# Two mixers in one transformer kernel: MoBA heads in pairs, row broadcasts through DRAM, and new SBUF addresses

## The chip, the cores and the metric

One core of one Trainium2 chip runs one program. The metric is the device time in microseconds of one execution; lower is better.

## What is computed

The reference is two transformer blocks of one layer each, in float32, on one sequence of 256 tokens of width 1024. Cut to what matters here:

```python
# first block
h = rmsnorm(x, norm_mix_pre)
proj = h @ w_in                                   # queries, keys, values, gates of three mixers
ya = gla_mixer(...) @ w_branch_a
yb = pool_mixer(...) @ w_branch_b
yc = moba_mixer(mq, mk, mv) @ w_branch_c          # 8 heads of width 64, causal attention with a
                                                  # linear bias; one block of 256 keys, so no selection
mixed = gs0 * ya + gs1 * yb + gs2 * yc            # gs = sigmoid(gates)
x = x + rmsnorm(mixed @ w_out);  x = x + rmsnorm(ffn(rmsnorm(x)))
# second block: three scans instead
y_hg = hgrn2_scan(...)                            # 8 heads of width 128
h_ml = mlstm_scan(q, k, v, i_pre, log_f)          # 4 heads; weights exp(bh[t] - bh[s] + ih[s] - m[t])
y_ssd = ssd_scan(xs, dt, A, Bm, Cm)               # 16 heads; weights exp(cum[t] - cum[s])
mixed = g0 * (y_hg @ w_br_hg) + g1 * (y_ml @ w_br_ml) + g2 * (y_mb @ w_br_mb)
x = x + mixed @ w_out;  x = x + ffn(rmsnorm(x));  return rmsnorm(x)
```

The scans are computed over all 256 tokens at once, as masked products, and not chunk by chunk.

## The kernel before

**Weights and precision.** All weights stream from HBM in pieces of 128 x 2048 words, one load each on SyncE's queue (two raw buffers, `wr`). ScalarE rounds each piece to float32r (`wh`), VectorE subtracts to get the rest (`wl`); there are three buffers of each. Every large product is three float32r matmuls: high by high, high by low, low by high (`three`). The normed input is held the same way, as `hhi` and `hlo`. Projections whose result is wanted channel-major (`proj_cm`) hold the weights stationary and move 256 tokens; those wanted token-major (`proj_tm`) hold the input stationary and move 512 weight columns. Their results are written to PSUM tiles `pp`; a piece is 48 matmuls of 256 columns or 24 of 512. `fetch` issues the loads and splits of a piece two pieces ahead of its use.

**Background work.** The mixers are Python generators. After each piece, `tick` advances every running generator to its next `yield`, so a mixer's small matmuls (PSUM tiles `m`, four banks) stand on TensorE between two weight pieces, one step a tick. They are plain float32, which TensorE does in two records each, with a transpose as one. TensorE works in the order in which the program is written, with few exceptions; VectorE and ScalarE are reordered by the scheduler that builds the program. Generators started earlier tick first.

**MoBA** (`moba`) runs next to the last projections and the gates of block 1. For head h, `scores` multiplies 64 channels of q and k (heads of even number lie on partitions 0 to 63, odd ones on 64 to 127, of one tile) into one bank: 128 columns for the first 128 queries, 256 for the rest. VectorE adds the bias and takes the row maxima, ScalarE the exponentials with their sums, VectorE divides. `turn` transposes the three 128 x 128 blocks and ScalarE copies them out. `values` multiplies by v, 64 output channels, into half of the partitions of a bank that two heads share. The loop runs `values(i - 2)`, `turn(i - 1)`, `scores(i)` in one tick, ten ticks for eight heads.

**mLSTM and SSD** (`mlstm`, `ssd`) run in block 2, mLSTM next to the projections for the output gate and SSD's input, SSD next to the gates and branches h and m. `rows` makes the running sums with time along the row, one head per partition, splits them into high and low parts in one tile `rowB`, and transposes another copy into columns. For each head `row_bc` then broadcasts one row to all partitions by a matmul: the stationary operand is one column of the 0/1 matrix `selr`, spread to 128, the moving one `rowB`, 256 columns. `causal_w` adds the column value to that PSUM tile, takes the minimum with a mask and then the exponential, in a 384-wide SBUF tile (`w1(384)`, four buffers that MoBA, mLSTM and SSD share). SSD handles two heads in a tick, and multiplies each head's weights with the inputs one tick later. A head's three products in mLSTM have 257 columns, in SSD 64.

**Addresses.** A partition of SBUF is one range of bytes; the address modulo 128 is called the residue below. Pools are laid out one after another in the order in which they are opened: constants, weights, big buffers, work tiles. The weight buffers are 2144 words (67 x 128 bytes) and all begin at residue 32. The ten big buffers (`b8`) are 2056 words, that is 64 x 128 + 32 bytes, so each begins 32 further than the one before it: 32, 64, 96, 0 and so on. `hhi` and `hlo` are the first two work tiles and begin at 96. A row of 256 tokens is 1024 bytes, so a slice keeps its tile's residue. The branch inputs Y, the split activations of the FFN and a few split weight pieces (`BIG`) lie in big buffers: Y of branch c at 64, b at 32, a at 64, h and m at 0 and 64, s at 0 and 96; of the `BIG` pieces that the FFN begins with, one at 96 and one at 32.

**POOL's queue** carries a few memsets, single-column powers, and loads: the bias, the pooling weights and the gains.

Of the kernel before, what the change touches and what calls it, by code (L numbers as in the profile page):

```python
# [8 lines left out]
F32 = mybir.dt.float32  # L9
# [7 lines left out]
T = 256  # L17
# [9 lines left out]
NBIG = 10  # L27
PP = 4
# [14 lines left out]
def _const_arrays():  # L43
# [16 lines left out]
    sel = np.zeros((128, 20))  # L60
    for h in range(4):
        sel[h, h] = sel[32 + h, h] = -1.0
    for h in range(16):
        sel[64 + h, 4 + h] = sel[96 + h, 4 + h] = 1.0
    parts["sel"] = sel
# [73 lines left out]
PW = 2144  # L139
PIECES = []  # L140
# [93 lines left out]
class Prog:  # L234
    def __init__(self, ctx, tc, A):
# [3 lines left out]
        self.wp = e(tc.tile_pool(name="wp", bufs=3))  # L239
        self.big = e(tc.tile_pool(name="big", bufs=NBIG))  # L240
        self.wk = e(tc.tile_pool(name="wk", bufs=2))
        self.pp = e(tc.tile_pool(name="pp", bufs=PP, space=bass.MemoryType.PSUM))
        self.mx = e(tc.tile_pool(name="mx", bufs=8 - PP, space=bass.MemoryType.PSUM))
# [16 lines left out]
    def b8(self, dt=F32, w=2048):  # L260
        return self.big.tile([128, 2056], dt, tag="b8", name=self.name("b"))[:, :w]
# [72 lines left out]
    def setup(self):  # L334
# [5 lines left out]
        self.selr = self.cp.tile([128, 20], F32R, name="selr")  # L340
# [7 lines left out]
        self.ident = self.c("ident")  # L348

# [53 lines left out]
    def load_consts(self):  # L403
        self.act(self.selr, self.c("sel"))
# [12 lines left out]
    def buffers(self, n):  # L417
# [4 lines left out]
        return (raw, *(self.wp.tile([128, PW], F32R, tag=g, name=f"{g}{n}", bufs=WBUF[g]) for g in ("wh", "wl")))  # L422
# [198 lines left out]
    def new_h(self):  # L621
        def one(nm):
            t = self.wk.tile([128, 2048], F32R, tag=nm, name=self.name(nm), bufs=1)
            return t.rearrange("p (k t) -> p k t", k=KT)
        return one("hhi"), one("hlo")
# [151 lines left out]
    def moba(self, q, k, v, alibi, OH, OL):  # L777

        nc = self.nc
        prob, turned, po = {}, {}, {}  # L780
        two = (slice(0, 128), slice(128, 384))

        def scores(h):
            c, p, slope = h // 2, slice(64 * (h % 2), 64 * (h % 2) + 64), 2.0 ** -(h + 1)
            sc = self.ps()
            self.mm(sc[:, 0:128], q[p, c, 0:128], k[p, c, 0:128])
            self.mm(sc[:, 128:384], q[p, c, 128:256], k[p, c, 0:256])
            s = self.w1(384)
            m = self.w1(8)
            self.tt(s, sc[:, :384], alibi, ALU.add)  # L790
            for t in range(2):
                nc.vector.tensor_reduce(out=m[:, t:t + 1], in_=s[:, two[t]], axis=AX.X, op=ALU.max)
# [739 lines left out]
```

## Time and profile before

| | us |
|---|---|
| median of 3 runs | 1058.92 |
| lowest, highest | 1057.8, 1063.15 |
| profiled execution, whole | 1060.68 |
| its span, first to last instruction | 1058.4 |
| TensorE (PE) busy | 1042.7 |
| VectorE (DVE) busy | 752.7 |
| ScalarE (ACT) busy | 605.8 |
| GpSimd (POOL) busy | 18.1 |
| granted TensorE clock, mean | 0.997 of full speed |

An engine's busy time is the time in which at least one of its instructions is open. TensorE's matmuls overlap, and their ends are modelled, so the busy share is not a share of its peak; the distance from one start to the next is what a matmul costs. Times in the rows are from the start of the span.

### The profile page before, as it was taken

The page shows a single profiled execution, that of the slowest core. Times are in us where ns is not written, and L with a number is a line of the kernel's source. Part 1 is how long each engine was busy: PE and PEld are TensorE (multiplying, and loading weights), DVE is VectorE, ACT ScalarE, POOL GpSimd, SP SyncE. Part 2 cuts the span into 40 slices and gives each one's busy share as a digit, 9 for nine tenths or more (in the row PEclk, how much of TensorE's full clock was granted, in tenths as well). Part 3 has the DMA queues.
Part 4 walks back from the last instruction along what each step waited for, and adds up shares of the span by engine and source line. Part 5 has one row for each costly group of instructions (what it writes and reads, how often), then busy time and mean ns, then how long its engine had stood idle before and what let it go on. Part 6 is the DMA issues. An engine that isn't in the chain of part 4 may idle for free.

```text
span 1058.4 us, 21256 instructions
## 1 busy us (share of the span) xinstructions
PE 1042.7 (99%) x8768; PEld 970.3 (92%) x8768; DVE 752.7 (71%) x1472; ACT 605.8 (57%) x1265; POOL 18.1 (2%) x29
## 2 busy tenths in 40 slices
PE   8999999999999999999989999999999999999997
PEld 7898899989999988799879899999999989999885
DVE  5766677687655545766888879977776686999753
ACT  7656455466554435655458656754565566776542
POOL 1000000001000000200000000000000000000000
PEclk9999999999999999999999999999999999999999
DMA  8643345555555546455425344454445554555561
GB/s 307 228 174 131 121 160 200 173 192 206 187 200 181 207 158 210 159 200 202 139 106 199 127 153 165 166 194 153 160 149 195 191 202 173 172 204 192 181 214 40
DMA packets 29936, 187.13 MB, mean 177 GB/s; under 512 B 3472, under 2 KB 4768, under 8 KB 8848
## 3 DMA queue, kind: packets, MB, share of 16 engines
q1 hardware_dynamic: 28544, 181.13, 49.0%
q0 software_dynamic: 720, 3.60, 0.9%
q8 instruction: 68, 1.11, 0.4%
q10 hardware_dynamic: 576, 1.05, 0.3%
q14 instruction: 28, 0.23, 0.1%
HBM read 184.72 MB, written 1.05 MB: 176 GB/s over the span
## 4 chain that ended last, share of the span: by engine, by line
PE 94%; DVE 2%; DMA 1%; ACT 1%; issue 1%; POOL 0%; SPq 0%; POOLq 0%; DVEq 0%; ACTq 0%
PE pp L298 86%; PE m L298 6%; DMA wr<-w 1%; DMA x<-x 1%; PE m L550 1%; DVE b L287 1%; PE m L617 0%; PE m L806 0%; POOL k L569 0%; ACT junk L564 0%; DVE wl L287 0%; ACT wh L284 0%; PE m L977 0%; DVE k L290 0%; ACT b L284 0%
## 5 line engine op out<-in xcount | busy, mean ns | idle before, releaser
L287 DVE TENSOR_TENSOR wl<-wr,wh 128x512 fp32r<-128x512 f32 (+2 forms) x660 | 424.2, 680 | 188.1 <-ACT wh L284 97.8
L284 ACT ACTIVATE wh<-wr 128x512 fp32r<-128x512 f32 (+2 forms) x660 | 373.3, 617 | 303.2 <-PE pp L298 273.6
L298 PE MATMUL pp<-hhi,wh 128*128 128x256 f32 x1440 | 199.9, 280 | 1.1 <-ACT hhi L284 1.0
L298 PE MATMUL pp<-hlo,wh 128*128 128x256 f32 x1440 | 194.8, 277 | 0.9 <-issue 0.9
L298 PE MATMUL pp<-hhi,wl 128*128 128x256 f32 x1440 | 194.2, 277 | 0.0
L298 PEld LDWEIGHTS pp<-hhi,wh 128*128 128x128 f32 x1440 | 180.0, 188 | 4.3 <-ACT hhi L284 2.1
L298 PEld LDWEIGHTS pp<-hlo,wh 128*128 128x128 f32 x1440 | 178.2, 188 | 1.1 <-issue 1.1
L298 PEld LDWEIGHTS pp<-hhi,wl 128*128 128x128 f32 x1440 | 178.1, 189 | 0.0
L298 PE MATMUL pp<-wh,b 128*128 128x512 f32 x512 | 131.2, 395 | 1.6 <-ACT wh L284 1.6
L298 PEld LDWEIGHTS pp<-wh,b 128*128 128x128 f32 x512 | 95.5, 188 | 24.4 <-ACT wh L284 1.7
L298 PE MATMUL pp<-b,wh 128*128 128x256 f32 x576 | 76.5, 282 | 0.0
L290 DVE SCALAR_TENSOR_TENSOR k<-pp,vecs,k 128x255 f32<-128x255 f32 (+1 forms) x148 | 70.2, 477 | 5.1 <-ACT k L284 3.7
L298 PEld LDWEIGHTS pp<-b,wh 128*128 128x128 f32 x576 | 71.6, 189 | 0.1
L298 PE MATMUL pp<-wl,b 128*128 128x512 f32 x256 | 71.3, 395 | 0.0
L298 PEld LDWEIGHTS pp<-wl,b 128*128 128x128 f32 x256 | 48.1, 188 | 11.4
L298 PE MATMUL pp<-wh,hhi 128*128 128x512 f32 (+3 forms) x232 | 52.4, 355 | 0.0
L298 PE MATMUL pp<-wh,hlo 128*128 128x512 f32 (+3 forms) x232 | 50.6, 348 | 0.0
L298 PE MATMUL pp<-wl,hhi 128*128 128x512 f32 (+3 forms) x232 | 50.4, 347 | 0.0
L298 PEld LDWEIGHTS pp<-wh,hlo 128*128 128x128 f32 x232 | 37.9, 188 | 6.1
L298 PEld LDWEIGHTS pp<-wl,hhi 128*128 128x128 f32 x232 | 37.9, 188 | 5.9
L284 ACT ACTIVATE k<-pp,vecs 128x256 f32<-128x256 f32 x62 | 34.4, 557 | 13.5 <-DVE k L290 8.7
L298 PEld LDWEIGHTS pp<-wh,hhi 128*128 128x128 f32 x232 | 37.0, 188 | 5.4 <-ACT k L284 0.3
(178 smaller groups left out, 929.3 us busy)
## 6 DMA issues: line engine op xcount, KB each, us to landing
wr<-w SPq DMA_DIRECT2D x158, 1024.0 KB, 4.8
wr<-w SPq DMA_DIRECT2D x10, 512.0 KB, 4.1
wr<-w SPq DMA_DIRECT2D x10, 256.0 KB, 4.7
wr<-w SPq DMA_DIRECT2D x2, 1072.0 KB, 4.9
wr<-w SPq DMA_DIRECT2D x2, 1056.0 KB, 4.9
b<-gains POOLq DMA_DIRECT2D x2, 1024.0 KB, 6.6
b<-xt SPq DMA_DIRECT2D x8, 128.0 KB, 4.3
x<-x SPq DMA_DIRECT2D x2, 512.0 KB, 6.7
```

The costliest lines, as they stand in the source:

```text
L284: return self.nc.scalar.activation(out=out, in_=in_, func=func, **k)
L287: return self.nc.vector.tensor_tensor(out=out, in0=a, in1=b, op=op)
L290: return self.nc.vector.scalar_tensor_tensor(out=out, in0=a, scalar=s, in1=b, op0=op0, op1=op1)
L298: return self.nc.tensor.matmul(out, lhsT=lhsT, rhs=rhs, start=start, stop=stop)
L550: self.nc.tensor.transpose(ps[:, k], part[:, 128 * k:128 * k + 128], self.ident)
```

## The change

**MoBA** works on pairs of heads. `scores(c)` issues the 256-column products of both heads one after the other, one on rows 0 to 63 and one on rows 64 to 127, each into its own bank, then the two 128-column ones. VectorE and ScalarE take the two heads in turn: both additions, then maxima and exponentials of each head, then the two divisions. `values(c)` alternates in the same way between the two halves of the output partitions. The loop has `values(i - 1)` and `scores(i)` in one tick and `turn(i)`, six transposes, in the next: nine ticks.

**Rows** are not split and not broadcast by TensorE. `rows` writes each set (4 rows, 16 rows) with two small DMAs from POOL's queue to a DRAM tile, 256 values and the last 128 of them again, and `row_bc` loads one row of 384 words into all 128 partitions, again from POOL's queue, into the `w1(384)` tile in which `causal_w` then works in place. The loads for the first two heads are issued when the mixer starts, later ones a step (mLSTM) or two heads (SSD) ahead of their use. `rowB`, `sel` and `selr` go, and mLSTM's rows are multiplied by -1.

**Addresses.** The big buffers are 2080 words (65 x 128 bytes), so all ten have the same residue; `hhi` and `hlo` move to a pool of their own behind them; two small pad tiles shift the pools. By the widths, the weights stay at 32 and big buffers, `hhi` and `hlo` all lie at 96.

```diff
@@ -25,6 +25,7 @@
...
 NBIG = 10
+BW = 2080
 PP = 4
...
@@ -57,12 +58,6 @@
...
     parts["lvl"] = np.concatenate([m.astype(np.float64) for m in lv], 1)
-    sel = np.zeros((128, 20))
-    for h in range(4):
-        sel[h, h] = sel[32 + h, h] = -1.0
-    for h in range(16):
-        sel[64 + h, 4 + h] = sel[96 + h, 4 + h] = 1.0
-    parts["sel"] = sel
     inv = np.zeros((128, 4, 16))
...
@@ -137,6 +132,7 @@
...
 PW = 2144
+WW = 2144
 PIECES = []
...
@@ -237,9 +233,12 @@
...
         self.wp = e(tc.tile_pool(name="wp", bufs=3))
+        e(tc.tile_pool(name="pd", bufs=1)).tile([128, 16], F32, name="padw")
         self.big = e(tc.tile_pool(name="big", bufs=NBIG))
+        self.hp = e(tc.tile_pool(name="hp", bufs=1))
         self.wk = e(tc.tile_pool(name="wk", bufs=2))
         self.pp = e(tc.tile_pool(name="pp", bufs=PP, space=bass.MemoryType.PSUM))
+        self.dp = e(tc.tile_pool(name="dp", bufs=1, space=bass.MemoryType.DRAM))
         self.mx = e(tc.tile_pool(name="mx", bufs=8 - PP, space=bass.MemoryType.PSUM))
...
@@ -258,7 +257,7 @@
...
     def b8(self, dt=F32, w=2048):
-        return self.big.tile([128, 2056], dt, tag="b8", name=self.name("b"))[:, :w]
+        return self.big.tile([128, BW], dt, tag="b8", name=self.name("b"))[:, :w]
 
...
@@ -337,7 +336,6 @@
...
         self.wg2 = self.cp.tile([16, 256], F32, name="wg2")
-        self.selr = self.cp.tile([128, 20], F32R, name="selr")
         self.mhalf = self.cp.tile([128, 16], F32, name="mhalf")
...
@@ -346,6 +344,7 @@
...
         self.ident = self.c("ident")
+        self.cp.tile([128, 8], F32, name="pad")
 
...
@@ -401,7 +400,6 @@
...
     def load_consts(self):
-        self.act(self.selr, self.c("sel"))
         self.ts(self.sg[:, 0:1], self.v("gla_norm"), 0.5, None, ALU.mult)
...
@@ -419,7 +417,7 @@
...
             return raw, self.b8(F32R), self.b8(F32R)
-        return (raw, *(self.wp.tile([128, PW], F32R, tag=g, name=f"{g}{n}", bufs=WBUF[g]) for g in ("wh", "wl")))
+        return (raw, *(self.wp.tile([128, WW], F32R, tag=g, name=f"{g}{n}", bufs=WBUF[g]) for g in ("wh", "wl")))
 
...
@@ -620,7 +618,7 @@
...
         def one(nm):
-            t = self.wk.tile([128, 2048], F32R, tag=nm, name=self.name(nm), bufs=1)
+            t = self.hp.tile([128, 2048], F32R, tag=nm, name=self.name(nm), bufs=1)
             return t.rearrange("p (k t) -> p k t", k=KT)
...
@@ -777,51 +775,66 @@
...
         nc = self.nc
-        prob, turned, po = {}, {}, {}
+        prob, turned = {}, {}
         two = (slice(0, 128), slice(128, 384))
-
-        def scores(h):
-            c, p, slope = h // 2, slice(64 * (h % 2), 64 * (h % 2) + 64), 2.0 ** -(h + 1)
-            sc = self.ps()
-            self.mm(sc[:, 0:128], q[p, c, 0:128], k[p, c, 0:128])
-            self.mm(sc[:, 128:384], q[p, c, 128:256], k[p, c, 0:256])
-            s = self.w1(384)
-            m = self.w1(8)
-            self.tt(s, sc[:, :384], alibi, ALU.add)
-            for t in range(2):
-                nc.vector.tensor_reduce(out=m[:, t:t + 1], in_=s[:, two[t]], axis=AX.X, op=ALU.max)
-            self.ts(m[:, 2:4], m[:, 0:2], -slope, None, ALU.mult)
-            for t in range(2):
-                nc.scalar.activation(out=s[:, two[t]], in_=s[:, two[t]], func=AF.Exp, bias=m[:, 2 + t:3 + t],
-                                     scale=slope, accum_out=m[:, 4 + t:5 + t])
-            nc.vector.reciprocal(out=m[:, 6:8], in_=m[:, 4:6])
-            for t in range(2):
-                self.ts(s[:, two[t]], s[:, two[t]], m[:, 6 + t:7 + t], None, ALU.mult)
-            prob[h] = s
-
-        def turn(h):
-            s = prob.pop(h)
-            tp = self.ps()
-            for j in range(3):
-                nc.tensor.transpose(tp[:, 128 * j:128 * j + 128], s[:, 128 * j:128 * j + 128], self.ident)
-            turned[h] = self.w1(384)
-            self.act(turned[h], tp[:, :384])
-
-        def values(h):
-            c, p = h // 2, slice(64 * (h % 2), 64 * (h % 2) + 64)
-            pt = turned.pop(h)
-            if h % 2 == 0:
-                po[c] = self.ps()
-            self.mm(po[c][p, 0:256], v[:, 0, 64 * h:64 * h + 64], pt[:, 0:256], stop=False)
-            self.mm(po[c][p, 128:256], v[:, 1, 64 * h:64 * h + 64], pt[:, 256:384], start=False)
-            if h % 2:
-                self.split(po.pop(c)[:, :T], OH[:, c], OL[:, c])
-
-        for i in range(MOBA_H + 2):
-            for f, h in ((values, i - 2), (turn, i - 1), (scores, i)):
-                if 0 <= h < MOBA_H:
-                    f(h)
+        rows = (slice(0, 64), slice(64, 128))
+
+        def scores(c):
+
+            sc = [self.ps() for _ in rows]
+            for o, qs, ks in ((two[1], slice(128, 256), slice(0, 256)), (two[0], slice(0, 128), slice(0, 128))):
+                for i, p in enumerate(rows):
+                    self.mm(sc[i][:, o], q[p, c, qs], k[p, c, ks])
+            ss, ms = [], []
+            for i in range(2):
+                s, m = self.w1(384), self.w1(8)
+                self.tt(s, sc[i][:, :384], alibi, ALU.add)
+                ss.append(s)
+                ms.append(m)
+            for i in range(2):
+                s, m, slope = ss[i], ms[i], 2.0 ** -(2 * c + i + 1)
+                for t in range(2):
+                    nc.vector.tensor_reduce(out=m[:, t:t + 1], in_=s[:, two[t]], axis=AX.X, op=ALU.max)
+                self.ts(m[:, 2:4], m[:, 0:2], -slope, None, ALU.mult)
+                for t in range(2):
+                    nc.scalar.activation(out=s[:, two[t]], in_=s[:, two[t]], func=AF.Exp, bias=m[:, 2 + t:3 + t],
+                                         scale=slope, accum_out=m[:, 4 + t:5 + t])
+            for i in range(2):
+                s, m = ss[i], ms[i]
+                nc.vector.reciprocal(out=m[:, 6:8], in_=m[:, 4:6])
+                for t in range(2):
+                    self.ts(s[:, two[t]], s[:, two[t]], m[:, 6 + t:7 + t], None, ALU.mult)
+            prob[c] = ss
+
+        def turn(c):
+            turned[c] = []
+            for s in prob.pop(c):
+                tp = self.ps()
+                for j in range(3):
+                    nc.tensor.transpose(tp[:, 128 * j:128 * j + 128], s[:, 128 * j:128 * j + 128], self.ident)
+                pt = self.w1(384)
+                self.act(pt, tp[:, :384])
+                turned[c].append(pt)
+
+        def values(c):
+            pts = turned.pop(c)
+            po = self.ps()
+            for t, o, ts in ((0, slice(0, 256), slice(0, 256)), (1, slice(128, 256), slice(256, 384))):
+                for i, p in enumerate(rows):
+                    h = 2 * c + i
+                    self.mm(po[p, o], v[:, t, 64 * h:64 * h + 64], pts[i][:, ts], start=t == 0, stop=t == 1)
+            self.split(po[:, :T], OH[:, c], OL[:, c])
+
+        n = MOBA_H // 2
+        for i in range(n + 1):
+            if i:
+                values(i - 1)
+            if i < n:
+                scores(i)
             yield
+            if i < n:
+                turn(i)
+                yield
 
...
@@ -1194,9 +1207,8 @@
...
         self.tt(R[32:36], Fc, g, ALU.add)
-        B = self.wk.tile([128, T], F32R, tag="rowB", name="rowB", bufs=1)
-        self.ts(B, R, 0.0, None, ALU.mult)
-        self.split(g, B[0:4], B[32:36])
+        self.ts(g, g, -1.0, None, ALU.mult)
+        self.row_ml = self.store_rows("rowm", g)
         yield
...
@@ -1208,7 +1220,7 @@
...
         self.act(R[96:112], dt)
-        self.split(cum, B[64:80], B[96:112])
+        self.row_ss = self.store_rows("rows", cum)
         yield
...
@@ -1218,21 +1230,27 @@
...
         self.act(em.rearrange("p (t h) -> p t h", t=2), cols[:, :, 32:36], AF.Exp, scale=-1.0)
-        self.rB, self.rcols, self.em = B, cols, em
+        self.rcols, self.em = cols, em
         yield
 
-    def row_bc(self, j):
-        ps = self.ps()
-        self.mm(ps[:, :T], self.selr[:, j:j + 1].to_broadcast([128, 128]), self.rB)
-        return ps
-
-    def causal_w(self, j, col):
+    def store_rows(self, name, src):
+
+        d = self.dp.tile([src.shape[0], T + 128], F32, name=name)
+        self.nc.gpsimd.dma_start(out=d[:, 0:T], in_=src)
+        self.nc.gpsimd.dma_start(out=d[:, T:], in_=src[:, 128:T])
+        return d
+
+    def row_bc(self, d, j):
+
+        w = self.w1(384)
+        self.nc.gpsimd.dma_start(out=w, in_=d[j:j + 1, :].to_broadcast([128, T + 128]))
+        return w
+
+    def causal_w(self, w, col):
 
         msk = self.c("cmask")
-        bc = self.row_bc(j)
-        w = self.w1(384)
-        for i, (a, b, c) in enumerate(((0, 256, 0), (256, 384, 128))):
-            self.stt(w[:, a:b], bc[:, c:256], self.rcols[:, i, col:col + 1], msk[:, a:b], ALU.add, ALU.min)
+        for i, (a, b) in enumerate(((0, 256), (256, 384))):
+            self.stt(w[:, a:b], w[:, a:b], self.rcols[:, i, col:col + 1], msk[:, a:b], ALU.add, ALU.min)
         self.act(w, w, AF.Exp)
...
@@ -1241,9 +1259,10 @@
...
         prob = {}
+        bc = {h: self.row_bc(self.row_ml, h) for h in range(2)}
 
         def scores(h):
-            w = self.causal_w(h, h)
+            w = self.causal_w(bc.pop(h), h)
             st = self.ps()
...
@@ -1268,6 +1287,8 @@
...
                 values(i - 1)
+                if i + 1 < 4:
+                    bc[i + 1] = self.row_bc(self.row_ml, i + 1)
             if i < 4:
...
@@ -1306,6 +1327,7 @@
...
                 yield
+        bc = {h: self.row_bc(self.row_ss, h) for h in range(2)}
         ss = self.wk.tile([128, 8], F32, tag="sss", name="sss", bufs=1)
...
@@ -1315,7 +1337,7 @@
...
                 self.mm(cb[g][:, 256:384], Bm[:, g, 128:256], Cm[:, g, 128:256])
-            w = self.causal_w(4 + h, 64 + h)
+            w = self.causal_w(bc.pop(h), 64 + h)
             self.stt(w, w, 0.25, cb[g][:, :384], ALU.mult, ALU.mult)
...
@@ -1339,6 +1361,9 @@
...
                     values(h)
+            for h in (i + 2, i + 3):
+                if h < 16:
+                    bc[h] = self.row_bc(self.row_ss, h)
             for h in (i, i + 1):
...
```

## Rows read from the trace of the kernel before

**Rows 1.** The page's busy time by engine: us, share of the span, instructions

```profile
PE 1042.7 (99%) x8768; PEld 970.3 (92%) x8768; DVE 752.7 (71%) x1472; ACT 605.8 (57%) x1265; POOL 18.1 (2%) x29
```

**Rows 2.** Waits of PE, whole run: us in total, times, longest

```profile
PE m L298 <- DVE b L287: 1.9, 2, 1.7
```

**Rows 3.** Timeline of PE, one MoBA step: start us, length us, engine, line, out<-in, count

```profile
85.83 0.86 PE L298 MATMUL m<-k,b 128*64 128x256 f32 x4
86.63 0.55 PE L806 MATMUL m<-const,k 128*128 128x128 f32 x3
87.11 0.92 PE L298 MATMUL m<-b 64*128 64x128 f32 x4
87.95 0.38 PE L298 MATMUL pp<-hhi,wh 128*128 128x256 f32 x1
```

**Rows 4.** Timeline of PE, a MoBA step with column quarters, then row halves in GLA

```profile
120.96 1.61 PE L298 MATMUL m<-b 64*128 64x128 f32 x68
122.49 0.39 PE L298 MATMUL pp<-hhi,wh 128*128 128x256 f32 x1
...
156.59 0.72 PE L298 MATMUL m<-b 64*128 64x128 f32 x8
157.24 0.70 PE L298 MATMUL m<-k,hold 128*128 128x256 f32 x2
```

**Rows 5.** Timeline of PE, an SSD step with broadcasts, and one without

```profile
727.30 1.45 PE L298 MATMUL m<-b,k 128*128 128x64 f32 x12
728.87 1.12 PE L298 MATMUL pp<-b,wh 128*128 128x256 f32 x8
...
779.44 1.45 PE L298 MATMUL m<-b,k 128*128 128x64 f32 x12
780.69 0.48 PE L298 MATMUL pp<-b,wh 128*128 128x256 f32 x2
```

**Rows 6.** Costliest groups of the page, branch matmuls with wh

```profile
L298 PE MATMUL pp<-b,wh 128*128 128x256 f32 x576 | 76.5, 282 | 0.0
```

**Rows 7.** Timeline of PE in the first FFN pieces, gates and branches

```profile
247.46 1.12 PE L298 MATMUL pp<-b,hlo 128*128 128x256 f32 x8
248.42 2.05 PE L298 MATMUL pp<-b,hhi 128*128 128x256 f32 x16
...
744.02 1.10 PE L298 MATMUL pp<-hhi,wh 128*128 128x256 f32 x8
...
746.85 1.10 PE L298 MATMUL pp<-hhi,wh 128*128 128x256 f32 x8
...
773.74 2.05 PE L298 MATMUL pp<-b,wh 128*128 128x256 f32 x16
...
799.51 1.16 PE L298 MATMUL pp<-hhi,wh 128*128 128x256 f32 x8
...
821.36 2.05 PE L298 MATMUL pp<-b,wh 128*128 128x256 f32 x16
...
844.00 1.33 PE L298 MATMUL pp<-wh,b 128*128 128x512 f32 x5
```

**Rows 8.** Timeline of DVE, one MoBA chain, and of PE at its next step

```profile
121.91 0.56 DVE L287 TENSOR_TENSOR k<-m,b 128x384 f32<-128x384 f32 x1 [0.34 <-PE m L298]
...
122.58 0.61 DVE L792 TENSOR_REDUCE k<-k 128x1 f32<-128x128 f32 x2
...
125.31 0.54 DVE L294 TENSOR_SCALAR k<-k,k 128x128 f32<-128x128 f32 x2
...
128.22 0.86 PE L298 MATMUL m<-k,b 128*64 128x256 f32 x4
```

**Rows 9.** DMA issues: out<-in, engine, count, KB each, median us to landing

```profile
hold<-wpool POOLq DMA_DIRECT2D x1, 256.0 KB, 4.4
b<-alibi POOLq DMA_DIRECT2D x1, 192.0 KB, 3.0
```

**Rows 10.** Waits of ACT, 600 to 830 us: us in total, times, longest

```profile
ACT wh L284 <- PE pp L298: 61.6, 28, 3.4
```

## The prediction

> **What bounds the kernel now.** I read the page's busy shares first, then PE's waits, then PE's own timeline stage by stage, because the first two leave nothing else. PE is busy for 1042.7 of 1058.4 us [rows 1], and the longest of PE's kinds of wait adds up to 1.9 us in the whole run [rows 2]. So the time is the sum of what PE's instructions cost: a change is worth the PE time that it takes out, less any wait that it brings to PE. A busy PE says little here, since matmuls overlap. I count from the start of one piece of the timeline to the start of the next, divided by its matmuls, and call that the pitch.
>
> **Part 1, MoBA in pairs.** One head now costs PE, in one tick: values 0.80 us (85.83 to 86.63), three transposes 0.48 (to 87.11), scores 0.84 (to 87.95), together 2.12 [rows 3]. Scores use 64 of the 128 rows, values 64 of the 128 columns, so half the array stands empty.
> Do two halves run at once when they are queued side by side? Two rows bear on it. The last GLA level (the 128-column products in decay_levels) queues two heads on rows 0 to 63 and then two on rows 64 to 127, each a 128-column fp32 product of two records, all close together: eight records take 0.65 us (156.59 to 157.24) [rows 4]. A head's scores are two 128-column and two 256-column records in one row half, six column units of 128 for 0.84 us, so eight units in one half would be some 1.1 us. They overlap. For column quarters: the piece at 120.96 holds a head's four score records (0.84) and 64 records of 32 columns on four quarters; it ends at 122.49, so the 64 took 0.69 us, 11 ns each, where a quarter of a 128-column record (a 256-column record is twice one, 0.84/6 = 0.14) is 35 ns. They overlap too [rows 4].
> In the new order the two heads' products stand next to each other, closer than in the GLA level. So a pair costs one head's values 0.80, one head's scores 0.84, and six transposes: 0.48 and three more at 0.11 (a 128-column record, 0.84/6 less the switches of the half array) make 0.81. That is 2.45 against 4.24 us, 1.79 a pair, **7.2 us** over four pairs. Lower bound, if halves don't overlap: the pair saves only the switches into and out of the half array, about 0.35 a pair, 1.4 us.
> What may be late next: a pair's transposes come one tick after its scores, as a head's did. The add on DVE starts at 121.91, the last scaling ends at 125.85, and PE comes back at 128.22 [rows 8]: 2.4 us to spare. A pair puts the second head's add (0.56) ahead of the first head's chain and its reductions (0.61) and scalings (0.54) into it, so the first head is done 0.6 to 1.2 later and the second up to 1.7 to 2.3. Values no longer stand ahead of the transposes (0.80 less to spare). That leaves between +1.0 and -0.7 us. Behind the waiting transposes stands all of PE. I take 0.4 a pair, **+1.5 us**, within 0 to 4.
>
> **Part 2, rows through DRAM.** It removes 20 broadcasts by PE (4 mLSTM heads, 16 SSD heads), each a 256-column matmul. A step of 12 value records and two broadcasts lasts 1.57 us (727.30 to 728.87); the same 12 without broadcasts 1.25 (779.44 to 780.69) [rows 5]: 0.16 each at most, and 0.11 at least, the pitch of a 256-column matmul [rows 7]. I take 0.12: **-2.4 us**. The splits of B and selr leave ACT and DVE, and one multiplication by -1 joins DVE: a few instructions off the path, nothing.
> It adds 4 small stores and 20 loads of 192 KB on POOL's queue. The nearest rows are the alibi load, 192 KB from that queue, 3.0 us to landing, and wpool, 4.4 [rows 9]. POOL has no other work in these stages that PE waits for. The two loads ahead of mLSTM and SSD are used in the tick that issues them: DVE stands for 3 to 4.4 us, and behind it the splits of weights and the evictions. What hides this is the lead of the weights: between 600 and 830 us ACT waits 28 times, 61.6 us, for PE to free a weight buffer [rows 10], so the splits run as far ahead as three buffers let them, two pieces of 5.5 us. Cost nothing; without that lead 2 x 4 = 8 us. Later loads: see the last rival.
>
> **Part 3, addresses.** The same 256-column matmul has two pitches. In the gates of branch s, with hhi/hlo (residue 96) moving and weights (32) stationary, 192 take 799.51 to 821.36: 113.8 ns. In the branch right behind, with Y at residues 0 and 96, 192 take 821.36 to 844.00: 117.9 [rows 7]. No background work runs in either. With background work (branch m, Y at 0 and 64) 48 take 773.74 to 779.44: 118.8 [rows 5, 7]. And where both operands lie at 96 (the split weights in a big buffer against hlo) 8 take 247.46 to 248.42: 120 [rows 7]. So the residue pair goes with the pitch, and 96 against 32 is the one that reaches 113.8.
> After the change all 864 branch matmuls (576 with wh [rows 6], half as many with wl) stand at 96 against 32. I give the 288 without background work (block 1's a, block 2's s) 4.0 ns. For the other 576 the rows leave a wide choice: behind an SSD step 24 gate matmuls at 96 against 32 took 744.02 to 746.85, 117.9 ns, so the clean pair can lose its pace for a while [rows 7]. I take 3.0 ns, between 118.8 - 117.9 and 118.8 - 113.8, nearer to the second since a step stands only once in 48: 1.15 + 1.73 = **-2.9 us**. Bounds: nothing, and 5.0 ns for all, 4.3 us. The 192 matmuls of split weights in big buffers all come to 96 against 96, some from 32: +0.2 us. Of the 512-column matmuls against a stationary big buffer (768) I have no row of a clean pair; bounds 0 and 4 ns (3 us), taken near nothing, -0.4.
> A rule stands against this part. The Trainium skill ("SBUF — State Buffer", Who interferes with whom) says that PE has two independent read ports, for the moving operand and for the weights, and never waits for anyone; no address enters. By it part 3 is worth nothing and the time would be about 1050.8. The trace's 113.8 beside 117.9 ns speaks against it.
>
> **Sum.** -7.2 + 1.5 - 2.4 - 2.9 + 0.2 - 0.4 = -11.2 us on a span of 1058.4. The profiled run took 1060.7 with 2.3 us outside the span; the median of the three runs is 1058.9, so I take the difference from that: 1047.7, say **1047.5 us**.
>
> **Rivals.**
> *The halves don't overlap, or the pair's chain is late* (the chain of part 1 at its far end). For it: reductions and exponentials of two heads share one DVE queue with the weight splits. Against it: the overlaps of [rows 4] and the 2.4 us of [rows 8]. Without overlap part 1 gives 1.4, with a chain late by 4 us 3.2, where the sum had 5.7: 1052 or 1050; both together -2.6, 1056. Chance 0.15, 0.02 of it for both.
> *Residues do nothing*: the two pitches belong to the stages (which buffers ACT and DVE write meanwhile), not to the address. For it: the 117.9 behind the SSD step. Against it: the 113.8 beside 117.9, both without background work. The sum loses 3.1 of its 11.2: 1050.8. Chance 0.10.
> *Everything is eaten by a new order*: DVE and ACT are reordered by the scheduler, and short waits on PE come back in the stages that it rearranges. PE's waits now are few, so they can only grow; 11 us over 40 pieces would be 0.3 a piece. 1055 to 1062. Chance 0.09.
> *The broadcast loads become the bound of SSD* (the other side). A head's buffer is one of four and is refilled two steps later. The circle is landing, chain on DVE and ACT (3.9 us as in [rows 8]), values (1.25 [rows 5]), and must fit two steps of 6.9 us (773.74 to 780.69 is one [rows 5, 7]), 13.8. With 4.4 to landing and a second load behind it, some 10.5: 3 us to spare. From about 8 us to landing the circle decides, and each us more costs one in each of four rounds; at 11 us the gain is gone, at 12.5 the kernel is slower by 0.5%: 1064 or more. The rows show 3.0 and 4.4, while SP's loads use the same 16 engines. The Trainium skill ("SBUF — State Buffer", the DVE-blocks-DMA trap) says that descriptors of a load from POOL's queue wait while DVE holds the port pair that the two share. That would lengthen just this landing; no run here shows such a wait. Chance 0.06.
>
> **How the numbers follow.** The forecast has 0.60. Faster by over 0.5% (5.3 us, about what a measurement here can tell from no change) means under 1053.6: 0.60 + 0.10 + 0.13 of the first rival = 0.83. Within: 0.02 + 0.08 = 0.10. Slower: 0.06 + 0.01 = 0.07. For the range: the far bounds of parts 1 to 3 with no late chain are -7.2 - 2.4 - 4.3 - 3 = -16.9, 1042; that all of it comes together is unlikely, so the range begins at 1042.5, and ends at 1054, which takes in the first two rivals.
>
> **What would show it.** Right: the branch of [rows 7] at a pitch near 114; pairs of scores and values as long as one head's now; no broadcast on PE; PE's waits still under 10 us in all; broadcast loads landing in 3 to 5 us. Wrong: transposes that begin with PE idle, released by DVE's last scaling; scores of a pair at 1.5 us; a branch still at 118; PE in 720 to 785 waiting for a scaled w.

## The result, and the profile after

| | before | after |
|---|---|---|
| median of four runs each, us | 1060.59 | 1047.32 |
| lowest, highest, us | 1057.8, 1063.15 | 1046.28, 1048.67 |
| profiled execution, whole, us | 1060.68 | 1046.28 |
| its span, us | 1058.4 | 1044.5 |

The ratio is 0.9876, 95% interval 0.9843 to 0.9909: faster by 1.2%. The forecast of 1047.5 is 0.2 us from the median, but two deviations cancel in that: the gain of the medians is 13.3 us where the sum had 11.2, and the kernel before stood at 1058.9 in the runs that the forecast started from.

The page of the changed kernel, busy time by engine, answers to [rows 1], its waits of PE to [rows 2] (us in total, times, longest):

```profile
PE 1028.7 (98%) x8748; PEld 961.5 (92%) x8748; DVE 749.5 (72%) x1470; ACT 602.8 (58%) x1262; POOL 31.1 (3%) x53
...
PE m L297 <- DVE b L286: 1.9, 2, 1.5
PE pp L297 <- ACT wh L283: 1.6, 1, 1.6
PE pp L297 <- ACT hhi L283: 1.6, 3, 1.1
```

PE's busy time fell by 14.0 us, the span by 13.9; the twenty instructions that went are the broadcasts. No kind of wait is over 2 us. PE is still the bound, so what follows is again a sum over its pieces.

A MoBA step now, PE's timeline (start us, length us, instructions), beside the step of one head in [rows 3]:

```profile
67.36 1.36 PE L814 MATMUL m<-const,k 128*128 128x128 f32 x6
...
74.39 0.87 PE L297 MATMUL m<-k,b 128*64 128x256 f32 x8
75.19 0.92 PE L297 MATMUL m<-b 64*128 64x256 f32 x8
76.05 0.48 PE L297 MATMUL m<-hold,wg 16*128 16x256 f32 x1
...
83.25 0.82 PE L814 MATMUL m<-const,k 128*128 128x128 f32 x6
83.83 0.36 PE L297 MATMUL pp<-hhi,wh 128*128 128x256 f32 x1
```

Read starts, not lengths. Values of two heads take 0.80 us (74.39 to 75.19) and their scores 0.86 (to 76.05), what one head took before (0.80 and 0.84). The four pairs' transposes have no idle time in front on PE, but the first pair's were held up: their row is 1.36 us long where the second pair's is 0.82, and among them the weight loads (PEld) waited for DVE's scaling:

```profile
68.01 0.46 PEld L814 LDWEIGHTS m<-const,k 128*128 128x128 f32 x3 [0.20 <-DVE k L293]
```

The six starts are spread over 1.08 us, those of each other pair over 0.55, so this pair lost about 0.5 us. The other three pairs lost nothing, nor did the first one in the second trace of the same kernel that is shown below.

The SSD step that had broadcasts in [rows 5], branch a and branch s:

```profile
730.51 1.45 PE L297 MATMUL m<-b,k 128*128 128x64 f32 x12
731.76 1.16 PE L297 MATMUL pp<-hhi,wh 128*128 128x256 f32 x8
...
202.52 1.11 PE L297 MATMUL pp<-b,wh 128*128 128x256 f32 x8
...
213.47 1.32 PE L297 MATMUL pp<-wh,b 128*128 128x512 f32 x5
...
807.71 1.46 PE L297 MATMUL pp<-b,wh 128*128 128x256 f32 x11
...
830.22 1.56 PE L297 MATMUL pp<-wh,b 128*128 128x512 f32 x6
```

The step lasts 1.25 us, as the one without broadcasts did. Branch a's 96 matmuls come at 114.1 ns ((213.47 - 202.52)/96), branch s's 192 at 117.2 ns, hardly below the 117.9 of [rows 7]: one step of the prediction that did not come true. The new loads (KB each, median us to landing), and DVE's wait for them between 590 and 790 us:

```profile
k<-rows POOLq DMA_DIRECT2D x16, 192.0 KB, 3.4
...
k<-rowm POOLq DMA_DIRECT2D x4, 192.0 KB, 4.5
...
DVE k L289 <- DMA k<-rows: 5.0, 4, 1.4
```

**Where the 13.9 us of the two spans came from.** I matched the starts of the `pp` matmuls of both traces, one by one in program order, and took the shift over each stretch (minus is faster; the sum is the 13.9 but for rounding):

| stretch of PE's work | us |
|---|---|
| start-up, before MoBA | -1.85 |
| the stretch with MoBA | -7.0 |
| split weights in big buffers (96 against 96 now) | +0.7 |
| 512-column products against big buffers, behind start-up | -0.8 |
| stretch with `rows` | -0.3 |
| mLSTM | -0.5 |
| SSD with branches h and m | -3.1 |
| branches c, b, a | -0.5, -0.3, -0.3 |
| branch s | -0.1 |
| gates of branch b | +0.1 |

The first line is no part of the change; 1.65 of it lies in one stretch of 10 us. Three windows of before, then the middle one of after (us, busy time and count of PE, PEld, DVE, ACT, POOL, then the granted clock, DMA share, GB/s):

```profile
31.00:34.70 3.70, 2.59 (x13) 1.73 (x13) 3.56 (x9) 3.70 (x10) 0.00 (x0) 1.00 0.34 85
34.80:38.10 3.30, 3.30 (x18) 3.30 (x17) 3.08 (x11) 2.25 (x6) 0.00 (x0) 0.50 0.54 228
38.20:42.00 3.80, 3.80 (x35) 3.80 (x35) 2.86 (x9) 2.30 (x5) 0.00 (x0) 1.00 0.88 298
```

```profile
34.80:38.10 3.30, 3.30 (x32) 3.30 (x31) 3.08 (x11) 2.25 (x6) 0.00 (x0) 1.00 0.58 216
```

In before's profiled execution TensorE ran at 1.2 GHz here (0.50 of 2.4), 18 matmuls where after has 32, behind 3.7 us in which it had waited for 1.1. After waited about as long (its PE was busy for 2.74 of those 3.70 us) and kept its clock. A second trace of the unchanged changed kernel, taken with the last experiments, has the same dip:

```profile
34.20:37.40 3.20, 3.19 (x15) 3.19 (x16) 3.20 (x7) 2.60 (x5) 0.00 (x0) 0.50 0.73 294
```

So either kernel can have it: eight of the fourteen traces here do (both kernels among them). The start-up of these two traces is 1.85 and 2.1 us longer than that of the changed kernel's first trace, 1.5 to 1.65 of it in the dip. In the comparisons below I say where one trace has it and the other not. How often it fell in the runs without a trace is not known, and so neither is its share in the medians.

### The profile page after: what moved, and what is told of

The parts are those of the page before. It is cut to its first block, busy times and chain, and to the rows that moved or that the text cites. A ratio compares the mean times of both kernels' runs of the same rounds, so it can differ in the third digit from the quotient of the medians.

```text
span 1044.5 us, 21285 instructions
## 1 busy us (share of the span) xinstructions
PE 1028.7 (98%) x8748; PEld 961.5 (92%) x8748; DVE 749.5 (72%) x1470; ACT 602.8 (58%) x1262; POOL 31.1 (3%) x53
## 3 DMA queue, kind: packets, MB, share of 16 engines
HBM read 188.65 MB, written 1.08 MB: 182 GB/s over the span
## 4 chain that ended last, share of the span: by engine, by line
PE 93%; DVE 2%; ACT 1%; issue 1%; DMA 1%; POOL 0%; SPq 0%; POOLq 0%; ACTq 0%; DVEq 0%
PE pp L297 86%; PE m L297 5%; DMA x<-x 1%; PE m L548 1%; DVE wl L286 1%; PE m L615 0%; DMA vecs<-vec 0%; ACT wh L283 0%; DVE b L286 0%; PE m L814 0%; POOL k L567 0%; ACT junk L562 0%; PE m L990 0%; ACT b L283 0%; DVE k L289 0%
## 5 line engine op out<-in xcount | busy, mean ns | idle before, releaser
L283 ACT ACTIVATE k<-pp,vecs 128x256 f32<-128x256 f32 x62 | 34.5, 558 | 15.8 <-DVE k L289 11.3
L283 ACT ACTIVATE k<-k 128x512 f32<-128x512 f32 (+2 forms) x47 | 26.9, 573 | 27.2 <-DVE k L289 22.3
```

What stands on the lines that cost most here:

```text
L283: return self.nc.scalar.activation(out=out, in_=in_, func=func, **k)
```

## The experiments

Twelve runs were made, one of them of the changed kernel again. Where one time is given, it is that of one execution, and the working is done on its trace, matched with that of the changed kernel (or of before) as above.

**1. Each part by itself.** Three kernels: before with only `moba` changed, before with only the rows changed, and the changed kernel without the addresses.

```diff
--- before, only moba() as changed                 (MoBA alone)
--- before, only rows/row_bc/causal_w/mlstm/ssd    (rows alone)
--- changed                                        (old addresses)
-BW = 2080
+BW = 2056
...
-        e(tc.tile_pool(name="pd", bufs=1)).tile([128, 16], F32, name="padw")
```

> The kernel before with MoBA in pairs alone. Theory (halves of the array overlap, the chain is in time): TensorE needs 6 to 7.5 us less between the first score block and the first branch, and nothing changes elsewhere; a pair's values take about 0.80 us and its scores about 0.85, as one head's did. Rival (no overlap, only fewer switches): 1 to 2 us less, scores of a pair 1.5 us. Rival (late chain): transposes start after idle time of TensorE, and the gain falls below 4 us.

> The kernel before with the rows through DRAM alone. Theory: 20 broadcasts of 0.12 us leave TensorE, 2.4 us less, some 0.5 in the mLSTM stretch and 1.9 in the SSD stretch. Rival (loads bind): the time is the same or longer, with TensorE idle before the products of SSD.

> The changed kernel with big buffers of 2056 words again, so that their residues run 32, 64, 96, 0, while weights stay at 32 and the normed input at 96. Theory: the six branch stages go back to 118 to 119 ns a matmul of 256 columns, and TensorE takes 2 to 3.5 us longer than in the changed kernel. Rival (residues do nothing): within 0.5 us of the changed kernel, and branch pitches as in it.

Measured: 1053.24, 1055.68 and 1048.52 us (before on the same chip 1057.08), spans 1051.2, 1053.9 and 1046.7. MoBA alone gained 7.2 us in its own stretch, 1.7 at the start (the dip), and lost 0.6 and 1.1 later, in the stretch of `rows` and around 870 us: 5.5 net of the dip. Rows alone gained 3.0 net of the dip, 1.1 of it in the stretch of `rows`, the rest in mLSTM and SSD. Most of the gain in the stretch of `rows` is waiting time of PE: the wait of 1.7 us of [rows 2] stands there and is 1.2 with rows alone (second line), and another of before's waits there (first line) is gone.

```profile
PE m L1216 <- ACT rowR L284: 0.4, 1, 0.4
```

```profile
PE m L299 <- DVE b L288: 1.2, 1, 1.2
```

Which of the instructions that went shortened them was not taken apart.

Without the addresses the changed kernel was 2.2 slower: branch c 0.4, b 0.3, a 0.3, h and m 1.2, the 512-column products 0.8, the gates of s 0.3, against 0.8 gained back on the split weights and about 0.3 in smaller shifts; branch s moved by 0.1. The parts add to 10.7. The changed kernel gained 12.1 without the start-up. Of the difference 1.1 is the loss of MoBA alone around 870 us, which the changed kernel does not have (the 0.25 that it lost there is the split weights'); 0.3 is open. So all three parts are real, and the one that was sized too high is the addresses.

**2. Is it the overlap of the halves?** The changed kernel with pairs made of two heads that lie in the same half of the partitions; the products and the number of steps are the same. The scores keep their order; the values, not in the cut, now come head after head.

```diff
+            p = rows[c % 2]
...
-                for i, p in enumerate(rows):
-                    self.mm(sc[i][:, o], q[p, c, qs], k[p, c, ks])
+                for i in range(2):
+                    self.mm(sc[i][:, o], q[p, 2 * (c // 2) + i, qs], k[p, 2 * (c // 2) + i, ks])
```

> The changed kernel with heads 0 and 2, 1 and 3 and so on as pairs, so that both heads of a pair use the same row half for scores and the same column half for values; ticks, counts and widths stay. Theory (the gain is overlap of the halves): a pair's scores take about 1.5 us where they took 0.86 and its values about 1.45 where they took 0.80, 5 us more in all. Rival (the gain is in fewer switches between shapes): under 1 us more.

Measured: 1053.51 us; the MoBA stretch is 4.7 us longer than in the changed kernel, 1.9 more is the start-up with the dip, and 0.6 is spread over the rest of the program. PE's timeline in the step that answers to 74.39 above:

```profile
76.52 1.51 PE L297 MATMUL m<-k,b 128*64 128x256 f32 x8
...
77.96 1.57 PE L297 MATMUL m<-b 64*128 64x256 f32 x8
...
79.46 0.69 PE L297 MATMUL m<-hold,wg 16*128 16x256 f32 x2
```

Values 1.44 instead of 0.80, scores 1.50 instead of 0.86: 1.28 a pair, 5.1 over four pairs. The same eight records take 0.86 us when neighbours alternate between the halves and 1.50 when they don't.

**3. Which distances give the fast pace?** First the normed input at other residues, in steps of 32 and then of 8 bytes off, one residue for each of its four uses (block 1, its FFN, block 2, its FFN).

```diff
+        o = (0, 8, 16, 24)[self.nh]      # second kernel: (2, 4, 30, 28)
...
-            t = self.hp.tile([128, 2048], F32R, tag=nm, name=self.name(nm), bufs=1)
+            t = self.hp.tile([128, 2080], F32R, tag=nm, name=self.name(nm), bufs=1)[:, o:o + 2048]
```

> The changed kernel with the normed input at another residue in three of its four uses: 96 in block 1 as before, 0 in the first FFN, 32 (that of the weights) in block 2, 64 in the second FFN. Theory (only 64 bytes between moving and stationary residue allow 113 to 114 ns): the 912 matmuls of 256 columns of the first FFN and those of the second go from 113.9 and 113.5 ns to 117 to 120, 3 to 5.5 us each, the 1536 of block 2 lose 3 to 7 us; 9 to 18 us longer in all. Rival (the pitch belongs to the stage, not to the address): under 1 us.

> As the run before, with residues 8 or 16 bytes away from 96: 104 in block 1, 112 in the first FFN, 88 in block 2, 80 in the second FFN. If the distance counts in steps of 32 bytes, 88 and 80 or 104 and 112 keep 113 to 114 ns and the others fall to 117 to 120, some 4 us an FFN; if it is gradual, each FFN lies between 114 and 118; if residues do nothing, the time stays within 1 us.

Measured: 1062.71 and 1071.72 us, 16.4 and 25.4 over the changed kernel's span. The first lies in its expected range; the second met none of its three cases, its FFNs coming at 118.6 and 118.8 ns and its last gates of block 2 at 120.8. But the larger tiles had also moved `hlo` away from `hhi`, from 8192 to 8320 bytes, and block 1 at the old residue 96 ran at 117.6 ns in the gates of branch a, where the changed kernel has 113.8. The two runs mix two causes. The next two take them apart: residue 96 kept and only the distance of the halves changed (block 1 8704 bytes, its FFN 8320, block 2 8448, its FFN 8576), then the residues 104, 0, 32 and 64 at the distance 8448.

```diff
...
-        return one("hhi"), one("hlo")
+        return one("hhi", 0, 2048), one("hlo", (128, 32, 64, 96)[self.nh], 2176)    # words
```

> The upper and lower half of the normed input keep byte residue 96, but the lower tile starts 512, 128, 256 and 384 bytes further from the upper one in block 1, its FFN, block 2 and its FFN (distances 8704, 8320, 8448 and 8576 bytes instead of 8192). Theory (the 113 ns pace is held across the change from one half to the other only if the two halves stand a power of two apart, and branch s, whose halves are 24960 bytes apart, stays at 117 for that reason): the FFN of block 1 goes from 113.9 to about 117 (912 matmuls, +2.5 to +3 us), the gates of s and the FFN of block 2 likewise (192 and 912 matmuls, +0.7 and +2.5 to +3 us), and block 1 at 512 shows whether a multiple of 512 is enough (gates of branch a at 113.8) or not (117); in all 5 to 8 us slower than the changed kernel. Rival (the residues modulo 128 alone set the pace, and s is slow for another reason): 113.5 to 114 ns everywhere, no change of time beyond 0.3 us, a start-up dip of the clock aside (1.7 to 1.9 us).

> The two earlier runs that moved the normed input to other residues had moved its halves 8320 bytes apart as well, an odd number of 128 bytes, so they mixed two causes. Here the halves stand 8448 bytes apart, an even number, and the residues are 104 in block 1, 0 in its FFN, 32 in block 2 and 64 in its FFN, against weights at 32. Theory (the pace needs both: operands 64 bytes apart modulo 128, and halves that agree modulo 256): the paces stay near those of the two earlier runs, about 120 ns (block 1's last gates), 118 to 119 (FFN of block 1), 119 (last gates of block 2), 117 to 118 (FFN of block 2), about 13 to 17 us slower than the changed kernel. Rival (the distance of the halves did it all, the residue nothing): 113.5 to 114 ns in all four, the time of the changed kernel. Between: a residue that falls to 114 alone is no matter of 64 bytes.

Measured: 1054.01 and 1069.34 us, 7.7 and 23.0 over the changed kernel's span (about 1.7 of each is the dip). PE's timeline inside the first FFN of the changed kernel, of the one with the distance 8320, and of the one with residue 0:

```profile
300.44 1.07 PE L297 MATMUL pp<-hhi,wh 128*128 128x256 f32 x8
301.35 1.07 PE L297 MATMUL pp<-hlo,wh 128*128 128x256 f32 x8
302.25 1.07 PE L297 MATMUL pp<-hhi,wl 128*128 128x256 f32 x8
303.16 0.28 PE L297 MATMUL pp<-hhi,wh 128*128 128x256 f32 x1
```

```profile
302.08 1.11 PE L297 MATMUL pp<-hhi,wl 128*128 128x256 f32 x8
303.02 1.10 PE L297 MATMUL pp<-hhi,wh 128*128 128x256 f32 x8
303.96 1.11 PE L297 MATMUL pp<-hlo,wh 128*128 128x256 f32 x8
304.91 0.87 PE L297 MATMUL pp<-hhi,wl 128*128 128x256 f32 x6
```

```profile
302.00 1.12 PE L297 MATMUL pp<-hlo,wh 128*128 128x256 f32 x8
302.96 1.11 PE L297 MATMUL pp<-hhi,wl 128*128 128x256 f32 x8
303.91 1.12 PE L297 MATMUL pp<-hhi,wh 128*128 128x256 f32 x8
304.86 0.88 PE L297 MATMUL pp<-hlo,wh 128*128 128x256 f32 x6
```

24 matmuls take 2.72, 2.83 and 2.86 us: 113.3, 117.9 and 119.2 ns. The means over whole stretches without background work, from the starts of neighbouring matmuls (weights at residue 32 in all of them):

| residue of the input | distance of its halves, bytes | stretch | ns |
|---|---|---|---|
| 96 | 8192 | FFNs of the changed kernel | 113.9, 113.5 |
| 96 | 8704 = 34 x 256 | block 1, last gates | 113.8 |
| 96 | 8448 = 33 x 256 | block 2, last gates | 113.8 |
| 96 | 8320 = 32.5 x 256 | FFN 1 | 117.3 |
| 96 | 8576 = 33.5 x 256 | FFN 2 | 117.3 |
| 64 | 8448; 8320 | FFN 2 | 117.8; 117.9 |
| 0 | 8448; 8320 | FFN 1 | 119.2; 119.0 |
| 32 | 8448; 8320 | block 2, last gates | 119.6; 119.1 |
| 104 | 8448; 8320 | block 1, last gates | 122.0; 121.3 |
| 112; 80 | 8320 | FFN 1; FFN 2 | 118.6; 118.8 |
| 88 | 8320 | block 2, last gates | 120.8 |

So among the addresses tried 113.5 needed both: the two operands 64 bytes apart modulo 128, and the two halves, between which PE goes to and fro every 8 matmuls, a multiple of 256 bytes apart. The first of the two expectations had said a power of two; 8448 and 8704 are none, and kept 113.8, so that the gates of s did not lose the 0.7 us expected there. The expectation for the last run, 13 to 17 us, was too low, mostly in block 1 at 104, where the background work runs too: 5.8 us were added there (7.5 with the dip). And branch s, whose halves lie in two big buffers three apart, 24960 = 97.5 x 256 bytes, lacks the second condition. Branches h and m have it: their old residues, 0 and 64, put their halves an even number of buffers apart, a multiple of 16640 = 65 x 256 bytes.

**4. The split weights at 32, and branch s mended.** First the `BIG` pieces 64 bytes into their buffers, which brings them from residue 96 to 32; then that and the upper half of branch s 128 bytes into its buffer (its halves are then 24832 or 25088 bytes apart, 97 or 98 x 256, by which of them stands first), timed in five rounds beside the changed kernel.

```diff
-            return raw, self.b8(F32R), self.b8(F32R)
+            return raw, self.b8(F32R, BW)[:, 16:2064], self.b8(F32R, BW)[:, 16:2064]
...
-        return tuple(self.b8(F32R).rearrange("p (k t) -> p k t", k=n) for _ in range(2))
+        return tuple(self.b8(F32R, BW)[:, i:i + 2048].rearrange("p (k t) -> p k t", k=n) for i in (o, 0))
...
-        Y.extend(self.r8())
+        Y.extend(self.r8(o=32))          # in ssd alone; o=0 elsewhere
```

> The changed kernel with the split weight pieces that live in big buffers moved 64 bytes into their buffer, to residue 32. Theory: the 192 matmuls of 256 columns between them and the normed input go from 120 ns (96 against 96) to 114 to 118: 0.4 to 1.1 us less. Rival (residues do nothing): the same within 0.2 us, and 120 ns as before.

> The changed kernel with two more steps of address: the split weights that lie in big buffers start 64 bytes into them (as in the earlier run, which was 2.6 us below the changed kernel without its start-up dip), and the upper half of branch s starts 128 bytes into its buffer, so that its halves stand 24832 or 25088 bytes apart, an even number of 128 bytes, where they stood 24960 apart. If the halves of one operand must agree modulo 256 for the 113 ns pace, branch s falls from 117.2 to about 114 ns (192 matmuls, -0.6 to -0.8 us), and the whole is 3.2 us below the changed kernel: about 1043 to 1045 us, ratio to the kernel before about 0.984. If something else keeps branch s slow it stays at 117, and the time is that of the split weights alone, about 1044 to 1046 us.

> The changed kernel itself, timed on the same chip beside the run with both steps: 1046 to 1049 us as before by every theory, branch s at 117.2 ns.

Measured: the split weights alone 1045.66 us in one run, with the dip in its trace. Both steps 1043.28 us (1043.02 to 1044.31), the changed kernel on the same chip 1047.83 (1047.07 to 1048.49); ratios to before (1060.54) 0.9838, 95% interval 0.9823 to 0.9852, and 0.9878, 0.9863 to 0.9892. The intervals don't meet: this version beats both kernels. Branch s in its trace, to be held against 807.71 and 830.22 above:

```profile
805.23 1.52 PE L297 MATMUL pp<-b,wh 128*128 128x256 f32 x12
...
826.99 0.86 PE L297 MATMUL pp<-wh,b 128*128 128x512 f32 x3
```

21.76 us for 192 matmuls, 113.3 ns where it had 117.2: 0.75 us, what the prediction had given this branch. The split weights gave 0.5 to 0.6 in the first FFN and nothing net in the second. Their own matmuls met both conditions now and yet went only from 119.8 to 117.8 ns in the first FFN. In the stretch of `rows` 1.2 to 1.4 us went besides, which I had not expected, and which is not the pace of a matmul: this idle time stands in both traces of the changed kernel (the first is shown), and in neither of the two with the split weights at 32.

```profile
528.89 0.50 PE L297 MATMUL pp<-hlo,wh 128*128 128x256 f32 x3 [1.06 <-issue]
```

Why it went is open ("issue" means that the profile shows nothing that PE waited for). In its trace against the changed kernel's first one (neither with the dip) the sum is 3.3 us: 0.75 for branch s, 0.6 for the split weights, 1.5 in the stretch of `rows`, and some smaller shifts, the transposes of the first MoBA pair among them. The medians differ by 4.5, and the other 1.2 I can't place. The dip would fit: the mean clocks on record are 0.998 to 0.999 in the five executions with both steps and 0.996 to 0.998 in the four beside them. So the paces are shown to give 1.3 us of the 4.5.

**5. Are the broadcast loads free?** Each load issued twice into the same buffer.

```diff
-        self.nc.gpsimd.dma_start(out=w, in_=d[j:j + 1, :].to_broadcast([128, T + 128]))
+        for _ in range(2):
+            self.nc.gpsimd.dma_start(out=w, in_=d[j:j + 1, :].to_broadcast([128, T + 128]))
```

> The changed kernel with each of the 20 broadcast loads issued twice into the same tile, so that a row lands about 3 to 4 us later. Theory (the circle of landing, chain and values has about 3 us to spare, and the weights' lead covers DVE's waits): within 1 us of the changed kernel. Rival (the loads are about to bind): 4 us longer for each us by which the landing passes 8 us, and TensorE idle before SSD's products.

Measured: 1057.6 us, 11.3 over the changed kernel's span; the 1 us or less that was expected is missed by far. 2.5 came in the stretch with mLSTM, 7.3 in that with SSD, 1.2 at the start (the dip). Its loads, its waits of DVE and of PE between 590 and 790 us, two rows of POOL, then PE's longest idle time and the windows behind it:

```profile
k<-rows POOLq DMA_DIRECT2D x32, 192.0 KB, 4.2
...
DVE k L289 <- DMA k<-rows: 26.8, 8, 6.3
...
PE m L297 <- DVE k L289: 6.5, 5, 3.0
...
740.56 0.54 POOL L1247 DMA_DIRECT2D k<-rows  x1 [4.22 <-DMA k<-rows]
743.50 1.59 POOL L1247 DMA_DIRECT2D k<-rows  x3 [2.40 <-DMA k<-rows]
...
751.53 0.88 PE L297 MATMUL m<-b,k 128*128 128x64 f32 x6 [3.02 <-DVE k L289]
...
753.00:756.30 3.30, 3.30 (x18) 3.30 (x18) 3.30 (x9) 1.44 (x5) 0.78 (x2) 0.50 0.66 117
756.50:760.00 3.50, 3.50 (x32) 3.50 (x32) 2.72 (x5) 2.09 (x5) 0.54 (x1) 1.00 0.92 297
```

A second load waits on POOL until the first has landed (the 4.22 us in brackets), so this run doubles more than the bytes: a head's landing is about twice 4.2 us, and the next load stands behind it. DVE then waited 26.8 us, PE 6.5, and the idle 3.0 us were followed by a second dip of the clock, 18 matmuls in 3.3 us where the next 3.5 hold 32. With single loads DVE waits 5.0 us and PE not at all. The loads cost nothing at 3.4 to 4.5 us; at about twice that they bind.

## Why the prediction was right, and where it was not

**Part 1.** -7.2 us for pairs: 7.0 in the changed kernel, 7.2 alone. The price of a step was right row by row (0.80 and 0.86 for a pair), and experiment 2 shows that the overlap of the halves makes 4.7 to 5.1 of it; the other 2 or so are what a pair saves without overlap, for which the prediction had 1.4. The chain "late by 0.4 a pair, +1.5" came to 0.5 for one pair in the first trace, nothing for its other three and nothing in the second trace. Why it is shorter than estimated was not tested.

**Part 2.** -2.4 us: 3.0 alone, of which about 2.1 in mLSTM and SSD, where the broadcasts were (20 x 0.11), and 1.1 in the stretch of `rows`. There the prediction had put the instructions that left DVE and ACT at "a few instructions off the path, nothing"; by experiment 1 PE waited 0.5 us less for DVE and 0.4 less for ACT without them. "Cost nothing" for the first loads was right: DVE waited 5.0 us in four times and PE in none. The threshold "from about 8 us to landing" agrees with experiment 5, though the expectation of that run put the doubled loads below it. Its slope, one us in four rounds for each more, was not measured.

**Part 3.** -2.9 + 0.2 - 0.4 = -3.1 us: -2.2 by experiment 1. The mis-sized term is "I give the 288 without background work 4.0 ns": right for branch a (3.4 ns), 0.7 for branch s. The cause is a condition that the prediction did not have. It read the pace off one residue pair; in its rows the gates that reached 113.8 had halves 8192 bytes apart as well, and no row of before shows residue 96 on both halves at another distance. Experiment 3 does, and experiment 4 gives branch s its 3.9 ns back. The other 576 were taken at 3.0 ns; h and m have 384 of them and gave 1.2 us, 3.1 ns, b and c (96 each) gave 3 to 4. The split weights at 96 against 96 cost 0.7 instead of 0.2, and the 512-column products gave 0.8 instead of 0.4.

A rule of the Trainium skill ("SBUF — State Buffer", Who interferes with whom) had it that PE's two read ports never wait for anyone, by which the addresses would be worth nothing. The traces disagree: the same 912 matmuls take 113.9 or 117.3 ns by the distance of two tiles alone.

**Rivals.** Without overlap the MoBA stretch would have gained under 3 us; it gained 7. Residues do something (2.2 us). A new order did not eat the gain. MoBA alone lost 1.7 us in later stretches, most of it idle time of PE; that a new order made them is not shown. Broadcast loads bind only when doubled.

**What was not foreseen.** The dip of the clock at start-up stands in the one trace of before that the sum was made against. Of the 13.9 us between the two spans 1.65 is that: the change itself is worth about 12 by the traces, where the sum had 11.2, and that the forecast lies 0.2 us from the median is luck.

## What to carry to other kernels

When PE is busy nearly all the time, price a change by the distance between starts of PE's rows, and check whether the profiled execution carries something, such as a stretch at half clock, that the other executions may not. Two products that each use half of the array are worth queuing alternately: here a pair then cost what one had. For long runs of matmuls look at the addresses of everything that alternates, not only of the two operands of one matmul, and vary one of them at a time, since a larger tile moves all that lies behind it.

## What the runs showed of the hardware

- A 256-column float32r matmul came at 113.3 to 113.9 ns, or at 117 to 122, by addresses alone. Among those tried, the lower pace needed the moving and the stationary tile 64 bytes apart modulo 128 and the two alternating moving tiles an even number of 128 bytes apart. 104 bytes against 32 was the slowest tried (121 to 122 ns). Why these distances is open.
- Both conditions met is not yet the low pace: in the gates among SSD steps the mean is 115.5 to 117.1 ns with input and distance as in the FFN, and the split weights moved to 32 came at 117.8 in the first FFN.
- TensorE's granted clock fell from 2.4 to 1.2 GHz right behind waits of the engine, at start-up in eight of fourteen traces (before's, and one of two of the changed kernel, among them) and once behind an idle 3.0 us in SSD; waits like those at start-up also passed without it.
